# Branch a and c merge logits and all eight gates in Strassen pairs after the convolution, kept in DRAM; branch b merged head by head

## The chip, the cores and the metric

The kernel runs on one core of one Trainium2 chip. The metric is the device time of one execution in microseconds (us). The engines are called as in the profile: PE is the matrix engine, DVE the vector engine, ACT the scalar engine, POOL the general engine (GpSimd), and SP the engine that issues all DMAs of this kernel.

## The reference

One step of a two-layer trunk over 640 tokens (128 context, 512 latent) with 1024 features. Each layer projects the normalised input with one wide matrix, runs three token mixers next to each other, and merges them with a sigmoid gate per channel:

```python
hmod = _rmsnorm(x, norm_g) * (1.0 + scale) + shift
(qa, ka, va, ga, z, xbc, dt_raw, qc, kc, vc, gc, merge) = split(hmod @ w_in)
# a: differential attention, 4 heads   b: Mamba-2 SSD, both directions   c: neighbourhood attention, 8 heads
ma, mb, mc = jnp.split(jax.nn.sigmoid(merge_logits), 3, axis=-1)          # 3 x 1024 logits per token
merged = (ma * ((ya * silu(ga)) @ w_br_a) + mb * (yb @ w_br_b)
          + mc * ((yc * silu(gc)) @ w_br_c))
x = x + gate * (merged @ w_out)
```

The gates `ga` and `gc` have 512 features each; `xbc` goes through a depthwise convolution of five taps before the SSD.

## The kernel before

Features lie on the 128 partitions and tokens on the free axis. Every float32 operand of a large product is kept as a rounded high part and a low rest, and a product is three matmuls (high by high, high by low, low by high). The normalised input is `self.h`, eight pairs of tiles of 128 features by 640 tokens. `feat` computes 128 output features for 640 tokens: two halves of 320 tokens, eight tiles of the contraction, three matmuls each, so 48 matmuls of 128x128 by 320 columns. Its weights come through `weights`: one DMA of 512 KB, a rounding copy on ACT (line 144) and a subtraction on DVE (line 145). `tok` does the same with tokens on the partitions, for values and for z.

A layer runs in five stages. In the convolution stage (`ssd`, lines 562 to 624) PE makes six tiles `xbc`, DVE runs five taps over each (line 609) and the SiLU (line 614), and PE transposes the result (lines 619 and 621). The SSD stage follows: z and dt by `tok`, then the scan in chunks, which writes branch b's output into `self.y`. Then come differential attention (`diff_kq`, `diff_attn`, one head after the other), neighbourhood attention (`na_vkq`, `na_ctx`, `na_head`, two heads at a time), and the tail with the merges of branch c, the output projection and the next norm.

The merge logits are made by `logit`, 48 matmuls for each of 24 tiles per layer, with a tanh, and `logits` spills them to the DRAM tensor `thd`. `merges` reads them back and multiplies them with the branch projection of `self.y`. The tables L1, LA, L2, LC say next to which head the logits of a and c are computed, MA where the merges of branch a stand; all merges of branch b stand at head 0. `gate_in` computes one gate tile (48 matmuls) for each head of a and each pair of heads of c.

A scheduler sets the order of instructions on each engine. It walks the program with priorities in program order and its own idea of each instruction's length, and takes what is ready and has a buffer. On the chip each engine then runs its own list strictly in that order. PSUM has three buffers `mm` for projections; the scores `s` of differential attention have one buffer of three banks, those of neighbourhood attention two.

## Time and profile before

| what | value |
|---|---|
| median of 3 runs | 1656.31 us (1655.13 to 1660.32) |
| the profiled execution | 1660.38 us, its span 1658.6 us |
| PE busy | 1598.4 us, 96% of the span |
| DVE busy | 1061.9 us, 64% |
| ACT busy | 770.3 us, 46% |
| POOL busy | 153.5 us, 9% |
| share of the chain that ended last | PE 79%, DMA 9%, DVE 5%, ACT 3% |

The profile is one execution on the chip. A matmul's record covers its whole passage through the array, so records of neighbouring matmuls overlap and the distance between starts is what one costs. The clock column is the granted clock of PE as a share of 2.4 GHz: 1.00 is 2.4 GHz, 0.50 is 1.2 GHz. Instruction lines (L170) are those of the kernel before.

### The profile page before, as it was taken

How to read it: one execution, taken by the hardware profiler on the slowest of the kernel's cores; microseconds unless marked ns; L12 is line 12 of the kernel's file. 1: busy time of each engine (PE TensorE's matmuls, PEld its weight loads, DVE VectorE, ACT ScalarE, POOL GpSimd, SP SyncE). 2: the span in 40 equal slices, each digit the busy share in tenths (PEclk: the TensorE clock that was granted, in tenths of full speed). 3: DMA queues.
4: the chain of work that ended last, by engine and by line, in shares of the span. 5: the costliest groups of instructions: out<-in, count | busy, mean ns of one | idle time of the engine just before them, and what ended most of it. 6: DMA issues, size and time to landing. Idle time of an engine off the chain costs nothing.

```text
span 1658.6 us, 28802 instructions
## 1 busy us (share of the span) xinstructions
PE 1598.4 (96%) x11166; PEld 1502.9 (91%) x11166; DVE 1061.9 (64%) x2287; ACT 770.3 (46%) x1776; POOL 153.5 (9%) x170
## 2 busy tenths in 40 slices
PE   4999999999999999999999999999999999999997
PEld 2998898999989888889989989999999898999997
DVE  4886767657536565566688668766665374667565
ACT  3647633345445454443456565334444354554432
POOL 0005210101000000000000242201010000000000
PEclk9999999999999999999999999999999999999998
DMA  9422235322265745557542222352222846445553
GB/s 304 124 86 74 83 124 159 99 79 79 75 121 138 159 129 148 165 189 270 172 138 85 82 82 86 118 190 69 72 85 76 158 139 122 111 126 167 198 165 128
DMA packets 114824, 214.61 MB, mean 129 GB/s; under 512 B 36736, under 2 KB 52608, under 8 KB 114688
## 3 DMA queue, kind: packets, MB, share of 16 engines
q1 hardware_dynamic: 114688, 212.78, 44.1%
q8 instruction: 88, 1.44, 0.4%
q14 instruction: 48, 0.39, 0.1%
HBM read 170.27 MB, written 34.08 MB: 123 GB/s over the span
## 4 chain that ended last, share of the span: by engine, by line
PE 79%; DMA 9%; DVE 5%; ACT 3%; issue 3%; SPq 1%; POOL 1%; POOLq 0%; DVEq 0%; ACTq 0%
PE mm L170 54%; PE mm L182 7%; DMA raw<-in_w_feat 2%; PE s L908 2%; PE t L924 2%; PE o L932 2%; PE o L493 2%; PE ada L242 1%; DMA qd<-qr 1%; PE s L478 1%; DMA aw<-in_w_ada 1%; DVE lo L145 1%; PE g L735 1%; ACT hi L144 1%; PE y L748 1%
## 5 line engine op out<-in xcount | busy, mean ns | idle before, releaser
L170 PE MATMUL mm<-hh,hi 128*128 128x320 f32 x1856 | 579.6, 313 | 4.4 <-ACT hh L317 4.4
L170 PE MATMUL mm<-hl,hi 128*128 128x320 f32 x1856 | 580.0, 313 | 2.2 <-DVE hl L318 2.2
L170 PE MATMUL mm<-hh,lo 128*128 128x320 f32 x1856 | 576.0, 311 | 0.5 <-DVE lo L145 0.5
L170 PEld LDWEIGHTS mm<-hh,hi 128*128 128x128 f32 x1856 | 351.0, 189 | 22.4 <-issue 11.5
L170 PEld LDWEIGHTS mm<-hl,hi 128*128 128x128 f32 x1856 | 350.8, 189 | 9.8 <-DVE hl L318 3.6
L170 PEld LDWEIGHTS mm<-hh,lo 128*128 128x128 f32 x1856 | 351.2, 189 | 6.4 <-issue 4.1
L145 DVE TENSOR_TENSOR lo<-raw,hi 128x1024 fp32r<-128x1024 f32 (+2 forms) x194 | 234.4, 1209 | 147.0 <-ACT hi L144 145.3
L144 ACT ACTIVATE hi<-raw 128x1024 fp32r<-128x1024 f32 (+2 forms) x194 | 200.1, 1033 | 231.2 <-PE mm L170 120.2
L170 PE MATMUL mm<-yh,hi 128*128 128x320 f32 x384 | 120.7, 316 | 7.3 <-DVE th L976 5.6
L170 PE MATMUL mm<-yl,hi 128*128 128x320 f32 x384 | 120.1, 313 | 0.2 <-DVE yl L338 0.2
L170 PE MATMUL mm<-yh,lo 128*128 128x320 f32 x384 | 119.1, 310 | 0.0
L487 ACT ACTIVATE ph<-t 128x384 fp32r<-128x384 f32 x64 | 31.3, 488 | 128.3 <-PE t L485 128.3
L182 PE MATMUL mm<-hi,hl 128*128 128x264 f32 (+1 forms) x320 | 90.7, 284 | 0.0
L182 PE MATMUL mm<-lo,hh 128*128 128x264 f32 (+1 forms) x320 | 90.6, 284 | 0.0
L182 PE MATMUL mm<-hi,hh 128*128 128x264 f32 (+1 forms) x320 | 90.4, 284 | 0.1
L170 PEld LDWEIGHTS mm<-yh,hi 128*128 128x128 f32 x384 | 72.7, 190 | 12.2 <-DVE th L976 7.6
L170 PE MATMUL mm<-mgl,hi 128*128 128x320 f32 x256 | 78.6, 308 | 0.0
L170 PE MATMUL mm<-mgh,lo 128*128 128x320 f32 x256 | 78.3, 308 | 0.1
L170 PE MATMUL mm<-mgh,hi 128*128 128x320 f32 x256 | 77.4, 306 | 0.0
L437 DVE TENSOR_REDUCE st<-s 128x2 f32<-128x1536 f32 (+1 forms) x40 | 59.5, 1487 | 26.0 <-PE s L478 24.9
L170 PEld LDWEIGHTS mm<-yl,hi 128*128 128x128 f32 x384 | 73.0, 190 | 0.8 <-DVE yl L338 0.4
L170 PEld LDWEIGHTS mm<-yh,lo 128*128 128x128 f32 x384 | 73.2, 191 | 0.0
(286 smaller groups left out, 2893.0 us busy)
## 6 DMA issues: line engine op xcount, KB each, us to landing
raw<-in_w_feat SPq DMA_DIRECT2D x110, 512.0 KB, 3.7
raw<-in_w_ada SPq DMA_DIRECT2D x32, 512.0 KB, 4.2
raw<-in_w_out SPq DMA_DIRECT2D x32, 512.0 KB, 3.7
thd<-th SPq DMA_DIRECT2D x48, 320.0 KB, 2.2
th<-thd SPq DMA_DIRECT2D x48, 320.0 KB, 3.8
raw<-in_w_br SPq DMA_DIRECT2D x24, 512.0 KB, 3.5
accd<-th SPq DMA_DIRECT2D x32, 320.0 KB, 3.5
ac<-accd SPq DMA_DIRECT2D x32, 320.0 KB, 4.6
```

What stands on the lines that cost most here:

```text
L144: nc.scalar.activation(hi, raw, AF.Copy)
L145: nc.vector.tensor_tensor(out=lo, in0=raw, in1=hi, op=ALU.subtract)
L170: nc.tensor.matmul(ps, lhsT=s, rhs=r, start=(k == 0 and n == 0), stop=(k == K - 1 and n == 2))
L182: nc.tensor.matmul(ps, lhsT=s, rhs=r, start=(k == 0 and q == 0), stop=(k == 7 and q == 2))
L242: nc.tensor.matmul(ps[32 * g:32 * g + 32, :], lhsT=self.sc[:, k, :], rhs=raw[:, 256 * g:256 * g + 256], start=(k == 0), stop=(k == 7))
L437: nc.vector.tensor_reduce(out=st[:, 0:2], in_=s, axis=AX.X, op=ALU.max)
L478: nc.tensor.matmul(s[:, m * 768 + c0:m * 768 + c0 + 512], lhsT=q[:, qs], rhs=ks[m][:, c0:c0 + 512], start=(i == 0), stop=(i == 1))
L487: nc.scalar.activation(ph[dst], pt[:, 0:3, :], AF.Copy)
L493: nc.tensor.matmul(ov[:, 0:256], lhsT=x[:, kt, sv], rhs=q[:, kt, :], start=(kt == 0 and n == 0), stop=(kt == 5 and n == 2))
L908: nc.tensor.matmul(s[:, c0:c0 + n], lhsT=q[:, i * 128:(i + 1) * 128], rhs=ks[j][:, k0:k0 + n], start=(x == 0), stop=(x == 1))
L924: nc.tensor.transpose(pt[:, t, :], e[:, t * 128:(t + 1) * 128], self.ident)
L932: nc.tensor.matmul(out, lhsT=lw, rhs=sel(q), start=(first and x == 0), stop=(last and x == 1))
```

## The change

Two logit tiles or gate tiles at a time are computed by Strassen's seven half-size products. The 2x2 blocks are the two feature tiles by the two halves of the contraction, and the two halves of tokens. `combine` builds, once per layer, the four combinations of `self.h` that the products need: `self.ut` (in the buffers of `self.y`) and `self.u2`. `pair` makes seven products of 12 matmuls each for two tiles, where before two calls of `feat` made 96 matmuls. Its weights are combined on DVE (lines 361 to 363 of the new file) and split in seven blocks; the products accumulate in three PSUM banks, with sums in between on DVE (lines 402, 408 and 412).

`ahead` makes all pairs of a layer in one go, 16 logit tiles of a and c and 8 gate tiles. It is called in `ssd`, behind the convolution and before z. The results go to `thd`, which has a fourth part for gates. `gate_in` now loads a gate from there. The tables L1, LA, L2, LC and their calls are gone. The merges of branch b are spread over the heads of differential attention by MB, two tiles at each. Since the merges of b now read `self.y` until head 3, the four outputs of branch a are held and written to `self.y` together (`last`). The SSD pool moves to the left side of SBUF, and the pool of the values `dv` opens behind `ahead`.

```diff
-L1 = (0,)
-LA = ((), (1, 2), (3,), (4, 5, 6, 7))
-L2 = ()
-LC = ((0,), (1,), (2, 3), (4, 5, 6, 7))
+MB = ((0,), (1,), (2,), (3,))
 MA = ((0,), (), (1,), (2, 3))
...
-        self.feat(self.w_in(l, c), self.h, evac)
+        self.dma(th, self.thd[3, i])
         return th
+
+    def combine(self, p):
+        self.ut = self.y
+        self.u2 = [tuple(p.tile([128, NT], F32R, name=f"u{s}{k}") for s in "hl") for k in range(4)]
+        for k in range(4):
+            f = []
+            for q in (k, k + 4):
+                hi, lo = self.h[q]
+                t = self.stage.tile([128, NT], F32, tag="ac", name="hf")
+                nc.gpsimd.tensor_tensor(out=t, in0=hi.bitcast(F32), in1=lo.bitcast(F32), op=ALU.add)
+                f.append((t[:, 0:320], t[:, 320:640]))
+            c = p.tile([128, 4, 512], F32, tag="sum", name="comb")...
+            u1, t3, u2, t4 = c[:, 0, 0:320], c[:, 0, 320:640], c[:, 1, 0:320], c[:, 1, 320:640]
+            nc.vector.tensor_tensor(out=u1, in0=f[0][0], in1=f[0][1], op=ALU.subtract)
+            nc.vector.tensor_tensor(out=t3, in0=f[1][1], in1=f[0][1], op=ALU.subtract)
+            nc.vector.scalar_tensor_tensor(out=u2, in0=u1, scalar=-1.0, in1=f[1][1], op0=ALU.mult, op1=ALU.subtract)
+            nc.vector.scalar_tensor_tensor(out=t4, in0=u2, scalar=-1.0, in1=f[1][0], op0=ALU.mult, op1=ALU.subtract)
+            for i, (hi, lo) in enumerate((self.ut[k], self.u2[k])):
+                nc.scalar.activation(hi, c[:, i], AF.Copy)
+                nc.vector.tensor_tensor(out=lo, in0=c[:, i], in1=hi, op=ALU.subtract)
+
+    def pair(self, l, c0, c1, p, done):
...
+        a00, a10, a01, a11 = (raw[:, i] for i in range(4))
+        sm = p.tile([128, 4, 512], F32, tag="sum", name="sum")
+        nc.vector.tensor_tensor(out=sm[:, 0:2], in0=raw[:, 0::3], in1=a01..., op=ALU.add)
+        nc.vector.tensor_tensor(out=sm[:, 2], in0=a00, in1=sm[:, 1], op=ALU.add)
+        nc.vector.tensor_tensor(out=sm[:, 3], in0=a10, in1=sm[:, 2], op=ALU.add)
...
+        product(b1, w1, self.h[0:4], lo_t, start=True)
+        p1 = copy("p1", b1)
+        product(b3, w5, self.ut, lo_t, start=True)
+        p5 = copy("p5", b3)
+        product(b2, w6, self.u2, lo_t, start=True)
+        nc.vector.tensor_tensor(out=b2, in0=b2, in1=p1, op=ALU.add)
+        u = copy("p6", b2)
+        product(b1, w2, self.h[4:8], lo_t, stop=True)
+        done(0, 0, b1, 1)
+        product(b2, w7, self.ut, hi_t)
+        nc.vector.tensor_tensor(out=c22, in0=b2, in1=p5, op=ALU.add)
+        done(1, 1, c22, -1)
+        product(b3, w3, self.h[4:8], hi_t, stop=True)
+        nc.vector.tensor_tensor(out=c12, in0=b3, in1=u, op=ALU.add)
+        done(0, 1, c12, 1)
+        product(b2, w4, self.u2, hi_t, stop=True)
+        done(1, 0, b2, -1)
...
             self.pre_end.close()
+            self.ahead(l)
+            vp = outer.enter_context(self.pool("dv"))
             p = es.enter_context(self.pool("ssd2"))
...
-                                if h == 0:
-                                    self.merges(l, 1, range(4), accd, first=True, spilled=range(8))
-                                g = self.gate_in(l, CA_G + 128 * h, cp)
-                                self.logits(l, 0, LA[h])
+                                self.merges(l, 1, MB[h], accd, first=True, spilled=range(8))
+                                g = self.gate_in(h, cp)
...
-                            g = self.gate_in(l, CC_G + 128 * hp, cp)
-                            self.logits(l, 2, LC[hp])
+                            g = self.gate_in(4 + hp, cp)
                             self.na_out(l, hp, y, g)
```

The order of instructions changes at three places. First PE (and DVE) at the end of layer 0's convolution. `hh` and `hl` are tiles of `self.h`, `t` and `g` the PSUM banks of the convolution's transposes. PE before:

```order
L170 MATMUL mm<-hl_96,hi 128x320
L170 MATMUL mm<-hh_95,lo 128x320
L619 MATMUL t<-masks,v 128x128 x4
L621 MATMUL g<-masks,v 128x128
L182 MATMUL mm<-hi,hh_81 128x264
L182 MATMUL mm<-lo,hh_81 128x264
L182 MATMUL mm<-hi,hl_82 128x264
L182 MATMUL mm<-hi,hh_83 128x264
```

PE in the changed kernel, from the first transposes on:

```order
L724 MATMUL t<-masks,v 128x128 x4
L726 MATMUL g<-masks,v 128x128
L724 MATMUL t<-masks,v 128x128 x4
L726 MATMUL g<-masks,v 128x128
L724 MATMUL t<-masks,v 128x128 x4
L726 MATMUL g<-masks,v 128x128
L724 MATMUL t<-masks,v 128x128 x4
L726 MATMUL g<-masks,v 128x128
L821 MATMUL w<-cf,bf 128x128 x2
L724 MATMUL t<-masks,bf 128x128 x4
L726 MATMUL g<-masks,bf 128x128
L386 MATMUL mm<-hh_81,hi 128x320
```

The projection of z (L182) stood between the transposes and now stands behind all twelve pairs. DVE in the changed kernel at the same place, where L719 ends the convolution and `comb` is the buffer of `combine`:

```order
L719 SCALAR_TENSOR_TENSOR v<-cth,v 128x640
L719 SCALAR_TENSOR_TENSOR bf<-cth,bf 128x640
L719 SCALAR_TENSOR_TENSOR cf<-cth,cf 128x640
L344 TENSOR_TENSOR comb<-hf 128x320
L345 TENSOR_TENSOR comb<-hf 128x320
L346 SCALAR_TENSOR_TENSOR comb<-comb,hf 128x320
L347 SCALAR_TENSOR_TENSOR comb<-comb,hf 128x320
L350 TENSOR_TENSOR yl_98<-comb,yh_97 128x640
L350 TENSOR_TENSOR ul_1073<-comb,uh_1072 128x640
L344 TENSOR_TENSOR comb<-hf 128x320
```

`combine` stands behind the convolution's last instruction, in both layers. The second place is PE in head 1 of differential attention in layer 0, behind one tile's scores `s`. Before:

```order
L478 MATMUL s<-ks,qh 128x512
L478 MATMUL s<-ks,ql 128x512
L170 MATMUL mm<-hh_93,hi 128x320
L170 MATMUL mm<-hl_94,hi 128x320
L170 MATMUL mm<-hh_93,lo 128x320
L170 MATMUL mm<-hh_95,hi 128x320
L170 MATMUL mm<-hl_96,hi 128x320
L170 MATMUL mm<-hh_95,lo 128x320
L170 MATMUL mm<-hh_81,hi 128x320
L170 MATMUL mm<-hl_82,hi 128x320
L170 MATMUL mm<-hh_81,lo 128x320
L485 MATMUL t<-masks,e 128x128 x3
```

Changed (L584 is the old L478, L591 the old L485; `rr` and `px` belong to the head's norm and context):

```order
L584 MATMUL s<-ks,qh 128x512
L584 MATMUL s<-ks,ql 128x512
L591 MATMUL t<-masks,e 128x128 x6
L624 MATMUL o<-masks,rr 10x128
L566 MATMUL o<-px,vx 128x128
L580 MATMUL s<-ks,qh 128x256
L580 MATMUL s<-ks,ql 128x256
L584 MATMUL s<-ks,qh 128x512
```

The projections between one tile's scores and the next one's are gone there. The third place is PE at the end of neighbourhood attention in layer 0, where `t` are transposes of the last tiles' weights `e` and `o` is the product with the values. Before:

```order
L170 MATMUL mm<-hh_93,hi 128x320
L924 MATMUL t<-masks,e 128x128 x4
L170 MATMUL mm<-hl_94,hi 128x320
L170 MATMUL mm<-hh_93,lo 128x320
L170 MATMUL mm<-hh_95,hi 128x320
L170 MATMUL mm<-hl_96,hi 128x320
```

Changed (L1016 is the old L908, L1032 the old L924, L1040 the old L932):

```order
L1040 MATMUL o<-pl,vs 128x128
L1016 MATMUL s<-ks,qh 128x128
L1016 MATMUL s<-ks,ql 128x128
L1016 MATMUL s<-ks,qh 128x128
L1016 MATMUL s<-ks,ql 128x128
L1016 MATMUL s<-ks,qh 128x256
L1016 MATMUL s<-ks,ql 128x256
L1032 MATMUL t<-masks,e 128x128 x16
L1040 MATMUL o<-ph,vs 128x512
```

The last head's transposes and scores follow each other with no projection between them.

## Rows read from the trace of the kernel before

**Rows 1.** Busy time of each engine in stretches; stretch, its length, busy (instructions), clock.
```profile
core 0: us, PE busy (x) PEld busy (x) DVE busy (x) ACT busy (x) POOL busy (x), PEclk, DMA share, GB/s
82.00:110.00 28.00, 28.00 (x234) 28.00 (x233) 26.12 (x59) 14.12 (x27) 0.00 (x0) 1.00 0.29 86
...
265.00:505.00 240.00, 231.51 (x1596) 220.06 (x1595) 140.19 (x262) 99.57 (x210) 21.16 (x15) 0.99 0.41 107
505.00:765.00 260.00, 254.35 (x1815) 231.57 (x1815) 148.88 (x381) 121.16 (x310) 1.58 (x1) 0.99 0.55 153
```
**Rows 2.** PE in order of time, end of xbc in layer 0; start, us, instruction.
```profile
81.62 0.31 PE L170 MATMUL mm<-hl,hi 128*128 128x320 f32 x1
81.76 0.31 PE L170 MATMUL mm<-hh,lo 128*128 128x320 f32 x1
81.91 0.60 PE L619 MATMUL t<-masks,v 128*128 128x128 f32 x4
```
**Rows 3.** The same for layer 1.
```profile
896.91 0.28 PE L182 MATMUL mm<-hi,hh 128*128 128x264 f32 x1
```
**Rows 4.** DVE's busy time on line 609 alone, layer 0 and layer 1.
```profile
83.00:110.00 27.00, 15.54 (x31) 1.00 0.29 88
897.00:912.00 15.00, 7.01 (x13) 1.00 0.18 54
```
**Rows 5.** The same for line 614.
```profile
83.00:110.00 27.00, 3.46 (x5) 1.00 0.29 88
897.00:912.00 15.00, 2.94 (x4) 1.00 0.18 54
```
**Rows 6.** Groups by line and shape: busy us, mean ns of one, idle before.
```profile
L286 DVE TENSOR_TENSOR acc<-acc,sq 128x320 f32<-128x320 f32 x42 | 20.5, 488 | 6.5 <-ACT sq L285 5.3
L338 DVE TENSOR_TENSOR yl<-of,yh 128x640 fp32r<-128x640 f32 x8 | 6.5, 818 | 4.5 <-ACT yh L337 4.5
L145 DVE TENSOR_TENSOR lo<-raw,hi 128x1024 fp32r<-128x1024 f32 x174 | 216.2, 1243 | 142.7 <-ACT hi L144 141.1 <-DMA accd<-th 0.9
L337 ACT ACTIVATE yh<-of 128x640 fp32r<-128x640 f32 x8 | 5.9, 740 | 11.9 <-POOL of L532 11.9
L144 ACT ACTIVATE hi<-raw 128x1024 fp32r<-128x1024 f32 x174 | 183.9, 1058 | 216.8 <-PE mm L170 108.5 <-DMA raw<-in_w_feat 66.2 <-DMA raw<-in_w_out 28.8
L532 POOL TENSOR_TENSOR of<-of,gate 128x640 f32<-128x640 f32 x8 | 16.8, 2104 | 95.1 <-ACT hi L144 67.0 <-DVE of L531 28.1
```
**Rows 7.** All engines in order of time, one tile's scores and softmax, differential attention.
```profile
408.54 0.91 ACT L440 ACTIVATE e<-s,st 128x768 f32<-128x768 f32 x1
...
410.09 1.02 DVE L444 SCALAR_TENSOR_TENSOR e<-e,st 128x768 f32<-128x768 f32 x1
...
413.61 0.28 PE L474 MATMUL s<-ks,qh 128*128 128x256 f32 x1
...
415.12 0.40 PE L478 MATMUL s<-ks,ql 128*128 128x512 f32 x1
415.56 1.76 DVE L437 TENSOR_REDUCE st<-s 128x2 f32<-128x1536 f32 x1 [3.25 <-PE s L478]
```
**Rows 8.** Groups by line and shape: softmax of neighbourhood attention on DVE.
```profile
L926 DVE TENSOR_TENSOR pl<-t,ph 128x512 fp32r<-128x512 f32 x64 | 43.6, 681 | 12.2 <-ACT ph L925 12.2
L921 DVE TENSOR_SCALAR e<-e,st 128x512 f32<-128x512 f32 x64 | 31.1, 486 | 1.9
L912 DVE CUSTOM_DVE_ANT_0 e<-s,bias 128x256 f32<-128x256 f32 x64 | 27.0, 421 | 46.7 <-PE t L924 27.9 <-PE t L889 10.6 <-PE s L908 7.8
L919 DVE TENSOR_TENSOR st<-st 128x1 f32<-128x1 f32 x64 | 10.1, 158 | 36.0 <-ACT e L918 35.3
```
**Rows 9.** Stretches of 5 us around one of PE's waits for a DMA.
```profile
1295.00:1300.00 5.00, 2.40 (x18) 1.99 (x17) 0.56 (x1) 2.79 (x11) 0.00 (x0) 0.96 1.07 181
1300.00:1305.00 5.00, 4.85 (x22) 4.04 (x23) 0.00 (x0) 0.00 (x0) 0.00 (x0) 0.50 1.42 103
1305.00:1310.00 5.00, 5.00 (x34) 4.99 (x34) 1.88 (x3) 2.79 (x6) 0.00 (x0) 0.85 1.22 162
```

More of the change, by code (lines that the diff above doesn't have):

```diff
@@ L319, in norm_part, with gate_in @@
                                                op1=ALU.subtract)
-    def gate_in(self, l, c, p):
-        nc = self.nc
-        th = p.tile([128, NT], F32, tag="gate", name="gate")
-        def evac(half, ps):
-            t = th[:, half * 320:half * 320 + 320]
-            nc.scalar.activation(t, ps, AF.Tanh, scale=0.5)
-            nc.vector.scalar_tensor_tensor(out=t, in0=t, scalar=1.0, in1=ps, op0=ALU.add, op1=ALU.mult)
-        self.feat(self.w_in(l, c), self.h, evac)
-        return th
+    def gate_in(self, i, p):
+        th = p.tile([128, NT], F32, tag="gate", name="gate")
+        self.dma(th, self.thd[3, i])
+        return th
@@ new lines, in combine @@
+    def combine(self, p):
+        nc = self.nc
+        self.ut = self.y
[7 more added lines that the diff above has]
+                f.append((t[:, 0:320], t[:, 320:640]))
+            c = p.tile([128, 4, 512], F32, tag="sum", name="comb").rearrange("p a n -> p (a n)")[:, 0:2 * NT]
+            c = c.rearrange("p (a n) -> p a n", a=2)
+            u1, t3, u2, t4 = c[:, 0, 0:320], c[:, 0, 320:640], c[:, 1, 0:320], c[:, 1, 320:640]
[6 more added lines that the diff above has]
+                nc.vector.tensor_tensor(out=lo, in0=c[:, i], in1=hi, op=ALU.subtract)
@@ new lines, in ahead, with done @@
+    def ahead(self, l):
+        nc = self.nc
+        with self.pool("ahead") as p:
+            self.combine(p)
+            jobs = [(C_M + 1024 * b + 128 * m, self.thd[b, m], 0) for b in (0, 2) for m in range(8)]
+            jobs += [(c + 128 * h, self.thd[3, o + h], 1) for c, o in ((CA_G, 0), (CC_G, 4)) for h in range(4)]
+            for i in range(0, len(jobs), 2):
+                ab = jobs[i:i + 2]
+                th = [self.stage.tile([128, NT], F32, tag="th", name="th") for _ in ab]
+                def done(m, half, v, sign):
+                    t = th[m][:, half * 320:half * 320 + 320]
+                    if ab[m][2]:
+                        nc.scalar.activation(t, v, AF.Tanh, scale=0.5)
+                        nc.vector.scalar_tensor_tensor(out=t, in0=t, scalar=1.0 * sign, in1=v, op0=ALU.add, op1=ALU.mult)
+                    else:
+                        nc.scalar.activation(t, v, AF.Tanh, scale=0.5 * sign)
+                self.pair(l, ab[0][0], ab[1][0], p, done)
+                for m in range(2):
+                    self.dma(ab[m][1], th[m])
@@ L533, in diff_out, with ssd @@
         self.dump(f"ya{l}_{h}", of)
-        self.put_y(h, of)
-    def ssd(self, l):
+    def ssd(self, l, outer):
         nc, a, o, sm = self.nc, self.a, self.o, self.sm
         with ExitStack() as es:
-            p = es.enter_context(self.pool("ssd"))
+            p = es.enter_context(self.pool("ssd", side="left"))
             pa = es.enter_context(self.pool("ps_a", space=PSUM))
@@ L783, in ssd @@
                     nc.vector.tensor_tensor(out=lo[:, tk], in0=yf[:, m], in1=hi[:, tk], op=ALU.subtract)
+            return vp
     def na_vkq(self, l, hp, p, pp, after_v=lambda: None):
@@ L1027, in build @@
             accd = dram.tile([8, 128, NT], F32, name="accd")
-            self.thd = dram.tile([3, 8, 128, NT], F32, name="thd")
+            self.thd = dram.tile([4, 8, 128, NT], F32, name="thd")
             src = a["x"]
@@ L1033, in build @@
             self.pre_end = ExitStack()
-            pre = self.pre_end.enter_context(self.pool("pre", side="left"))
+            pre = self.pre_end.enter_context(self.pool("pre"))
             with self.pool("x0") as xp, self.pool("aw0", bufs=9) as wp, self.pool("ps_a0", space=PSUM) as pp:
@@ L1066, in build @@
                 with ExitStack() as ph:
-                    with self.pool("dv") as vp:
-                        self.ssd(l)
+                    with ExitStack() as dv:
+                        vp = self.ssd(l, dv)
                         cp = ph.enter_context(self.pool("carry", side="left"))
@@ L1072, in build @@
                         self.logits(l, 1, range(8))
-                        self.logits(l, 0, L1)
                         with self.pool("diff") as p, self.pool("ps_d", space=PSUM) as ps:
@@ L1076, in build @@
                             kq = self.diff_kq(l, 0, p)
-                            pend = []
+                            pend, outs = [], []
                             for h in range(4):
@@ L1088, in build, with last @@
                                 d = self.diff_norm(att, cp, pp)
+                                outs.append(att[0])
                                 pend.append(lambda h=h, att=att, d=d, g=g: self.diff_out(l, h, att, d, g, sg, pp))
-                    self.logits(l, 2, L2)
                     with self.pool("na") as p, self.pool("ps_n", space=PSUM) as ps:
-                        vkq = self.na_vkq(l, 0, p, pp, lambda: pend and pend.pop()())
+                        def last():
+                            pend.pop()()
+                            for h in range(4):
+                                self.put_y(h, outs[h])
+                        vkq = self.na_vkq(l, 0, p, pp, last)
                         ys, gate, nxt = [], [], []
```

36 lines of the change are left out of this document (added).

## The prediction

> **What bounds the kernel now.** I read the busy times by stretch first. PE is busy in 28.00 of 28 us at the end of layer 0's convolution, in 231.51 of 240 us of differential attention and in 254.35 of 260 us of neighbourhood attention [rows 1]; DVE, the next one, has 140.19 and 148.88 us in the two attention stretches, under 60%. The kernel is bound by PE because every wait for DVE or ACT has a projection matmul standing in PE's list behind it. Then I read PE in order of time: neighbouring matmuls of 320 columns start 0.14 to 0.15 us apart [rows 2]; I take 0.146. Last I read what DVE does where the change takes PE's cover away.
>
> **What it removes.** A pair of tiles took 96 matmuls and takes 84. There are 12 pairs in a layer and two layers, so 24 x 12 = 288 matmuls go, 288 x 0.146 = **42 us** at most, all on the path. The splits move with them and grow: per pair seven blocks of 512 columns instead of four, plus the sums, about 8.4 us of DVE (3.5 x 1.24 for the low parts, 2.6 for the weight sums, three adds of 0.49 [rows 6]) beside 84 x 0.146 = 12.3 us of PE. DVE holds that pace, so this work alone is hidden by the pair's own matmuls.
>
> **What it moves, 1: the end of the convolution.** In the old order z's matmuls follow at once when the last xbc matmul is done, at 81.9 us in layer 0 [rows 2] and 896.9 us in layer 1 [rows 3]. In the new order only the convolution's transposes follow, and behind them the pairs, whose products with `ut` and `u2` need `combine`. On DVE `combine` stands behind the last convolution instruction. So PE waits for DVE's rest of the convolution, then for `combine`, then for the first weight sums.
>
> The rest of the convolution: after 83 us DVE still spends 15.54 + 3.46 = 19.0 us on it [rows 4, 5], in layer 1 after 897 us 7.01 + 2.94 = 10.0 us. Neighbouring records overlap a little, and z's splits no longer stand between, so I put its end at 101 us (99 to 103) and 905.5 us (904 to 908).
>
> `combine` has four rounds. A round needs two POOL adds of 640 columns; the nearest row is a POOL product of the same size, 2.10 us [rows 6]. Their buffers come free only when DVE has read the round before, so a round lasts about 2 x 2.1 = 4.2 us. Its DVE part (four operations of 0.49, two of 0.82) and ACT's 0.74 end 3 us behind the second add. Three rounds, 12.6, plus the last one's 4.2 make 17 us with the first adds partly hidden; then the weight sums (1.24 + 0.7) and their split (1.06), 3 us. In all 20 us (16 to 23) from the convolution's end to full pace. The Trainium skill (SBUF — State Buffer, "SBUF: two separate sides") says that POOL and a two-input DVE operation lock each other out of a shared port for a whole instruction. No run here shows POOL's add without DVE beside it; by that rule adds and DVE work would follow each other in a round of some 6 us, an estimate that would make the sum 7 us a layer longer.
>
> PE's work inside: five groups of transposes of about 0.45 us from the first start to the next instruction [estimated from rows 2: four start within 0.43], and the first pair's 24 products with `h`, 3.5 us; 6 us. So PE stands still for 101 + 20 - 82 - 6 = **33 us** in layer 0 and 905.5 + 20 - 897 - 6 = **23 us** in layer 1, together +56 (44 to 66). Nothing is gained back: z still has to be made afterwards, and the SSD scan begins only then.
>
> **The clock after that.** After a wait of 2.6 us before (5 us with 2.40 busy) the granted clock is 0.50, the level of 1.2 GHz, in the next 5 us and 0.85 in those behind [rows 9], a loss of 2.5 + 0.8 = 3.3 us. Part of it falls into the 24 products that wait anyway. Two times 2: +4 (0 to 8).
>
> **2: hand-overs inside the pairs.** Product 7 is added into the bank into which DVE has just added p1 and from which ACT copied p6; one or two products (1.75 or 3.5 us) stand between. The two operations take 0.5 + 0.4 us, but each can stand behind a split (1.24, 1.06 [rows 6]): 3.2 us. So 0 to 1.5 us per pair; the order of PE leaves two products between in half of the cases, I take 0.4: +10 (0 to 36).
>
> **3: differential attention without filler.** With gates and logits gone it has 4 x 48 + 7 x 48 = 528 matmuls less per layer, counted above as moved. What is left in PE's list is not spread: the projections for the next head all stand in heads 0 and 2, and heads 1 and 3 run nearly bare. Scores have one buffer, so the next tile's scores start when both exponentials have read it: scores 1.4 us (413.61 to 415.12 with three transposes between), the maximum 1.76, a small operation 0.2, two exponentials 2 x 0.9, hand-overs about 0.3 [rows 7], 5.5 us. PE's own work in a cycle is 1.4 of scores, 0.65 of transposes and 9 value matmuls of 256 columns, 1.05 (by 0.146 for 320): 3.1. Idle 2.4. The new list has six cycles per layer without filler (three in head 1, three in head 3), two context parts of 1.4, and at the end of head 3 the softmax and the last value product, about 6. With some waiting of DVE's list inside: **23 us** per layer, +46 (24 to 64).
>
> **4: neighbourhood attention without filler.** 576 matmuls less per layer. Per tile DVE takes 0.42 twice, 0.49, 0.68 and four small ones of 0.16 to 0.2 [rows 8], 2.6 us; PE 0.47 of scores, 0.43 of transposes, 0.47 of values, 1.4. Where no projection stands between, that is 1.2 idle per tile. In the new list about 14 of 32 tiles of a layer are bare, all eight of the last pair of heads among them, 17 us; then the chain from the last scores over the value product, the sum, the gate and `put_y` to branch c's merges, which need the last tile of `self.y`, some 6 us bare. 23 per layer, less 5 us of adaLN matmuls that stand in these gaps in layer 0 and the waits that the old kernel has anyway: +38 (16 to 60). Behind the new waits stand, on SP, the loads of weights in the same list as the gate loads; they are early, so I give them nothing.
>
> **The sum.** -42 + 56 + 4 + 10 + 46 + 38 = +112 on the profiled execution's 1660.4 us, 1772. The median of the runs is 4 us below that execution, so I predict **1768 us**.
>
> **Rivals.** *Only the convolution costs.* If DVE and ACT run the bare attention tiles faster than I read, or the remaining projections slip under them, terms 3 and 4 vanish: -42 + 56 + 4 = +18, 1674 us, with hand-overs up to 1690. Against it: the list has no projection in those places, and PE can't leave its list. For it: DVE is under 60% busy there. 12%.
>
> *The clock stays low.* In bare stretches PE works 3.1 of 5.5 us and 1.4 of 2.6. If it is held at 1.2 GHz there as in [rows 9], scores (1.4) and transposes take twice as long: +1.5 in the 12 bare cycles of both layers, +0.8 in the 28 bare tiles, and some 10 for the projections next to them that run slower too, together +50: 1818 us. The Trainium skill (TensorE: Matmul & The Clock Gate, "HAM oscillation — how this bites in real kernels") says that matmuls in bursts with waits between fall back to the low clock burst after burst, a rule against this change. The trace shows it once per long wait, and shows none for waits of 1 us. 18%.
>
> *Faster.* The 42 us arrive if `combine` runs under the xbc matmuls instead of behind the convolution: its inputs are ready, only its buffers and its place in the list hold it. Then the wait is DVE's convolution rest alone, 19 + 8 us less the 6 us of PE's work in each, some 16 us, and with bare attention hidden it would be -42 + 16 + 10 = -16, 1640 us. It decides below a wait of 42 us in sum. The list speaks against it: in both layers `comb` stands behind L719. 4%. That fewer matmuls are made than I count is no rival: the PE lists have 10697 and 10409 instructions of this kind.
>
> **How the numbers follow.** The forecast holds 66%. The range has to leave out no more than 2 in 10: from all terms near their low ends (-42 + 44 + 24 + 16 = +42, 1698) up to all but the last of the low-clock rival, 1835. So 1700 to 1835. A measurement tells 0.3%, about 5 us, from no change. Faster 0.04 (the last rival), the same 0.03 (the first rival with its wait at the low end), slower 0.93.
>
> **What would show it.** Right: PE idle for 25 to 40 us behind xbc in layer 0 and somewhat less in layer 1, ended by DVE's sums or ACT's split; PE waits for ACT's exponentials and DVE's or ACT's softmax in heads 1 and 3 and in the last pair of heads; the twelve pairs in 147 us a layer plus a few. Wrong: pairs that run well over 160 us (hand-overs), attention stretches that shrink by the full 77 and 84 us per layer (528 and 576 matmuls), or a busy PE between xbc and the first pair.

## The result and the profile after

The changed kernel takes 1869.85 us (median of 4 runs, 1865.44 to 1875.78) against 1658.32 us before (4 runs, 1655.13 to 1661.49): a ratio of 1.1278, 95% interval 1.1233 to 1.1323. Its profiled execution spans 1863.6 us, 205.0 us more than before. PE's page entry went from 1598.4 to 1640.7 us busy, although it makes 288 matmuls fewer (x11166 to x10878).

The windows view of the changed kernel, by stage: the end of the convolution with the pairs and the scan, differential attention, neighbourhood attention, first layer 0, then layer 1. Columns as in [rows 1].

```profile
82.40:418.80 336.40, 301.08 (x2065) 286.83 (x2064) 241.76 (x390) 173.21 (x370) 58.34 (x46) 0.94 0.29 99
418.80:635.10 216.30, 186.16 (x1155) 169.02 (x1153) 143.49 (x292) 85.50 (x182) 24.14 (x22) 0.87 0.29 88
635.10:872.20 237.10, 206.84 (x1363) 178.67 (x1362) 136.24 (x373) 107.20 (x295) 2.74 (x2) 0.90 0.61 152
997.40:1335.70 338.30, 311.58 (x2125) 297.46 (x2124) 240.13 (x389) 176.17 (x376) 58.61 (x46) 0.94 0.29 98
1335.70:1548.30 212.60, 181.79 (x1155) 165.77 (x1153) 145.03 (x291) 85.38 (x182) 24.97 (x22) 0.90 0.29 89
1548.30:1765.30 217.00, 186.94 (x1231) 169.18 (x1230) 135.54 (x368) 106.11 (x293) 2.74 (x2) 0.93 0.53 128
```

The same six stages of the kernel before, cut at the same instructions (bounds that [rows 1] doesn't have).

```profile
81.90:229.50 147.60, 147.60 (x1058) 136.37 (x1057) 109.03 (x231) 87.41 (x230) 41.07 (x38) 1.00 0.27 85
229.50:484.80 255.30, 249.44 (x1722) 238.67 (x1721) 161.88 (x312) 105.58 (x216) 28.03 (x22) 0.99 0.34 104
484.80:763.90 279.10, 270.82 (x1921) 246.66 (x1921) 154.33 (x393) 128.34 (x331) 2.75 (x2) 0.99 0.60 153
886.40:1043.40 157.00, 157.00 (x1122) 145.90 (x1121) 110.35 (x229) 90.56 (x237) 41.89 (x38) 1.00 0.26 81
1043.40:1297.50 254.10, 249.25 (x1722) 238.49 (x1720) 161.24 (x311) 105.53 (x216) 29.12 (x22) 0.99 0.34 104
1297.50:1560.50 263.00, 258.40 (x1806) 246.28 (x1807) 155.61 (x388) 127.62 (x329) 3.51 (x2) 0.98 0.54 133
```

Two things are to be read off. Length less busy time is PE's idle time: from 0 to 35.3 and 26.7 us in the first stage, from 5.9 and 4.9 to 30.1 and 30.8 us in differential attention, from 8.3 and 4.6 to 30.3 and 30.1 us in neighbourhood attention. And the busy time is longer than the matmuls in it: differential attention of layer 0 has 567 matmuls fewer, at 0.146 us 82.8 us, so 249.44 - 82.8 = 166.7 us were to be left, and it is 186.16. This excess is 19.5 and 15.3 us there, 17.5 and 12.5 us in neighbourhood attention, 6.5 and 8.1 us in the first stage. The clock column tells why: 0.87 to 0.94 where it was 0.98 to 1.00. A stage at 0.87 spent 2 x 0.13 = 26% of its time at the level of 1.2 GHz, 56 us of the 216.3 in differential attention of layer 0. PE was busy in 86% of that stage, and half of 0.86 x 56 is 24 us: an estimate from the clock column alone, near the 19.5 us of excess.

What PE waited for over the whole span (the waits view: us in total, times, longest):

```profile
PE mm L386 <- ACT hi L371: 29.9, 4, 11.4
PE t L724 <- DVE v L719: 23.1, 4, 12.8
...
PE t L1032 <- DVE st L1023: 14.1, 9, 2.5
PE t L591 <- DVE pl L594: 12.2, 8, 2.0
```

The first two are the end of the convolution; the others are transposes of attention that wait for the softmax or for the transposes ahead of them to be read. At the full clock the pairs run without a gap: in a stretch of 20 us inside them PE is busy 20.00 us with 140 matmuls, 0.143 us each.

```profile
145.00:165.00 20.00, 20.00 (x140) 20.00 (x139) 12.67 (x17) 10.23 (x20) 0.00 (x0) 1.00 0.49 171
```

### The profile page after: what moved, and what is told of

The parts are those of the page before. It is cut to its first block, busy times and chain, and to the rows that moved or that the text cites. A ratio compares the mean times of both kernels' runs of the same rounds, so it can differ in the third digit from the quotient of the medians.

```text
span 1863.6 us, 28849 instructions
## 1 busy us (share of the span) xinstructions
PE 1640.7 (88%) x10878; PEld 1518.3 (81%) x10878; DVE 1249.9 (67%) x2527; ACT 855.6 (46%) x1912; POOL 178.7 (10%) x186
## 5 line engine op out<-in xcount | busy, mean ns | idle before, releaser
L167 PE MATMUL mm<-hh,hi 128*128 128x320 f32 x1088 | 343.2, 316 | 8.6 <-ACT hh L314 4.5
L167 PE MATMUL mm<-hl,hi 128*128 128x320 f32 x1088 | 343.7, 316 | 2.1 <-DVE hl L315 2.1
L167 PE MATMUL mm<-hh,lo 128*128 128x320 f32 x1088 | 339.4, 312 | 0.2 <-DVE lo L142 0.2
L142 DVE TENSOR_TENSOR lo<-raw,hi 128x1024 fp32r<-128x1024 f32 (+2 forms) x146 | 176.2, 1208 | 85.1 <-ACT hi L141 83.9
L167 PEld LDWEIGHTS mm<-hh,hi 128*128 128x128 f32 x1088 | 208.6, 192 | 20.2 <-issue 5.9
L141 ACT ACTIVATE hi<-raw 128x1024 fp32r<-128x1024 f32 (+2 forms) x146 | 149.5, 1026 | 146.3 <-PE mm L167 62.6
L167 PEld LDWEIGHTS mm<-hl,hi 128*128 128x128 f32 x1088 | 208.4, 192 | 10.1 <-issue 3.9
L167 PEld LDWEIGHTS mm<-hh,lo 128*128 128x128 f32 x1088 | 208.5, 192 | 3.4 <-issue 1.5
L167 PE MATMUL mm<-yh,hi 128*128 128x320 f32 x384 | 120.4, 317 | 7.3 <-ACT yh L443 6.6
L386 PE MATMUL mm<-hh,hi 128*128 128x320 f32 x288 | 90.2, 313 | 8.9 <-ACT hi L371 7.1
L386 PE MATMUL mm<-hh,lo 128*128 128x320 f32 x288 | 90.2, 314 | 5.4 <-DVE lo L372 5.4
L386 PE MATMUL mm<-hl,hi 128*128 128x320 f32 x288 | 90.8, 316 | 0.0
L386 PE MATMUL mm<-yh,hi 128*128 128x320 f32 x192 | 60.6, 315 | 22.8 <-ACT hi L371 22.8
L371 ACT ACTIVATE hi<-sum 128x1024 fp32r<-128x1024 f32 x48 | 50.8, 1062 | 61.5 <-PE mm L386 54.8
L167 PE MATMUL mm<-mgl,hi 128*128 128x320 f32 x256 | 78.6, 308 | 0.0
```

Of the source, the lines that this page charges most:

```text
L141: nc.scalar.activation(hi, raw, AF.Copy)
L142: nc.vector.tensor_tensor(out=lo, in0=raw, in1=hi, op=ALU.subtract)
L167: nc.tensor.matmul(ps, lhsT=s, rhs=r, start=(k == 0 and n == 0), stop=(k == K - 1 and n == 2))
L371: nc.scalar.activation(hi, src, AF.Copy)
L386: nc.tensor.matmul(ps, lhsT=s, rhs=r, start=(start and k == 0 and n == 0), stop=(stop and k == 3 and n == 2), skip_group_check=True)
```

## The experiments

**Theory**, after these two traces: attention lost its filler (idle time, and a slow clock because of it), and `combine` is late; the pairs themselves are fine. **Rivals**: the pairs cost more than their matmuls; the merges by head do the harm; the excess of busy time isn't the clock. Medians are set against 1869.85 us; intervals are those of the ratio to the kernel before.

### The attention's filler: c_only and a_only

`c_only` gives the tiles of a back to differential attention, `a_only` those of c to neighbourhood attention.

```diff
-jobs = [... for b in (0, 2) for m in range(8)]
-jobs += [... for c, o in ((CA_G, 0), (CC_G, 4)) for h in range(4)]
+jobs = [... for b in (2,) for m in range(8)]
+jobs += [... for c, o in ((CC_G, 4),) for h in range(4)]
...
-g = self.gate_in(h, cp)
+g = self.gate(l, CA_G + 128 * h, cp)
+self.logits(l, 0, LA[h])
```

> The changed kernel with the logits of a and the four gates of a computed beside differential attention again, by 48 plain matmuls each and next to the same heads as in the kernel before; only the logits and gates of c are made in pairs behind the convolution (six pairs a layer instead of twelve). Merges of b stay spread over the heads. Theory: differential attention has its filler back, so its extra idle time (24.3 and 25.9 us) and its slow clock (19.5 and 15.3 us) go, 85 us, against 144 matmuls more, 21 us: about 1806 us (1790 to 1825). Rival: the loss in differential attention comes from spreading the merges of b over the heads: then nothing comes back and it is 1870 to 1890 us.

> The changed kernel with the logits and gates of c computed beside neighbourhood attention again, 48 plain matmuls each, next to the same pairs of heads as in the kernel before; only those of a are made in pairs behind the convolution (six pairs a layer). It is the counterpart of the run that gave a's back, which went from 1870 to 1796 us. Theory: neighbourhood attention gets back its extra idle time (22 and 25.5 us) and slow clock (17.5 and 12.5 us), 77 us, against 144 matmuls more, 21 us: 1813 us (1800 to 1830). Rival: neighbourhood attention is bound by its own chains also with the filler, since its tiles keep one buffer of transposes: 1850 us or more.

`c_only` took 1796.12 us (1.0745 to 1.0853), 74 us less; `a_only` 1807.71 us (1.0832 to 1.0936), 62 us less. The stage that got its tiles back, layer 0, first of `c_only` (differential), then of `a_only` (neighbourhood):

```profile
347.50:593.40 245.90, 240.07 (x1654) 230.61 (x1653) 159.27 (x311) 104.76 (x215) 26.43 (x22) 0.99 0.31 99
```

```profile
564.00:845.70 281.70, 272.03 (x1914) 248.16 (x1915) 154.26 (x393) 128.03 (x332) 2.74 (x2) 0.98 0.59 151
```

Idle time is back at 5.8 and 9.7 us, the clock at 0.99 and 0.98. Each run also makes 144 matmuls more (21 us), so the lost filler had cost 95 and 83 us. The traces alone gave 85 and 77.5 us (idle and excess together). For both stages it is shown that the lost filler is the cause.

### Strassen or the place: plain_ahead

```diff
-            self.combine(p)
...
-                self.pair(l, ab[0][0], ab[1][0], p, done)
+            self.feat(self.w_in(l, c), self.h, evac)
```

> The changed kernel without Strassen: the 24 tiles are still made behind the convolution, ahead of z, and kept in DRAM, but each by 48 plain matmuls, so combine and the pairs are gone. The rest (merges of b by head, attention without filler) is as in the changed kernel. Theory: 288 matmuls more (+42 us), while PE no longer waits at the end of the convolution, since the plain tiles need only self.h (62 us of waits and some 14 us of slow clock back): about 1835 us (1820 to 1850); what is left over the kernel before, about 175 us, is the attention stages alone. Rival: the pairs themselves cost more than their 84 matmuls (hand-overs between the seven products, DVE's seven splits): then it comes out below 1810 us.

1843.15 us (1.1034 to 1.1134). PE is idle for 1.7 us from the last xbc matmul to the end of the scan:

```profile
83.30:399.50 316.20, 314.46 (x2210) 302.89 (x2209) 147.24 (x272) 131.16 (x301) 43.03 (x38) 1.00 0.35 107
```

So moving the tiles costs 183 us without any Strassen, and Strassen, put in there, made it 27 us worse in place of 42 us better: its waits and their slow clock (62 + 15 us) eat the saving.

### The end of the convolution: z_first, combine_dve, spread_combine

```diff
+            for i in range(2):   # z_first: z's projections
+                w = [self.weights(a["w_z"][l, i, e], 4, 264) for e in range(2)]
+                ...
             self.ahead(l)
...
-                nc.gpsimd.tensor_tensor(out=t, in0=hi.bitcast(F32), ...)   # combine_dve
+                nc.vector.tensor_tensor(out=t, in0=hi.bitcast(F32), ...)
...
+            for c, dst, gate in jobs[:6]:   # spread_combine: both edits above, and
+                self.feat(self.w_in(l, c), self.h, evac)
+                self.dma(dst, t6)
+                next(rounds, None)          # one round of combine
```

> The changed kernel with one thing moved: z's and dt's projections stand ahead of the pairs again, as they stood behind the convolution in the kernel before. Nothing else differs. Theory: the end of the convolution costs what PE stands still there, 35.3 us in layer 0 and 26.7 us in layer 1, and some 14 us for the slow clock in the pairs behind it; z's 240 matmuls per layer cover DVE's rest of the convolution and the combination of self.h, so about 70 us come back: 1800 us (1790 to 1815), with PE busy from the last xbc matmul to the first pair. Rival: the wait is only put off, since z's splits and sums stand on DVE between the convolution and the combination, so the pairs wait then: 1830 to 1865 us with a wait of 10 us or more behind z.

1839.71 us (1.1025 to 1.1122): 30 us came back, not 70. The rival held. PE's waits from 80 to 300 us:

```profile
PE mm L386 <- ACT hi L371: 13.2, 2, 12.5
```

Why `combine` is still late there is seen in the changed kernel too. Its round in order of time (start, duration):

```profile
103.08 0.48 DVE L344 TENSOR_TENSOR comb<-hf 128x320 f32<-128x320 f32 x1
...
104.05 1.72 POOL L339 TENSOR_TENSOR hf<-hh,hl 128x640 f32<-128x640 f32 x1 [3.20 <-DVE comb L345]
104.41 1.71 DVE L347 SCALAR_TENSOR_TENSOR comb<-comb,hf 128x320 f32<-128x320 f32 x1
106.04 0.81 DVE L350 TENSOR_TENSOR yl<-comb,yh 128x640 fp32r<-128x640 f32 x1
106.26 1.99 POOL L339 TENSOR_TENSOR hf<-hh,hl 128x640 f32<-128x640 f32 x1 [0.50 <-DVE comb L347]
106.92 2.01 DVE L350 TENSOR_TENSOR ul<-comb,uh 128x640 fp32r<-128x640 f32 x1
109.04 0.49 DVE L344 TENSOR_TENSOR comb<-hf 128x320 f32<-128x320 f32 x1
...
110.25 3.16 DVE L372 TENSOR_TENSOR lo<-raw,hi 128x1024 fp32r<-128x1024 f32 x2
...
117.35 0.49 DVE L344 TENSOR_TENSOR comb<-hf 128x320 f32<-128x320 f32 x1
...
123.30 0.49 DVE L344 TENSOR_TENSOR comb<-hf 128x320 f32<-128x320 f32 x1
...
126.78 1.23 DVE L361 TENSOR_TENSOR sum<-raw 128x1024 f32<-128x1024 f32 x1
...
128.77 2.01 ACT L371 ACTIVATE hi<-sum 128x1024 fp32r<-128x1024 f32 x2 [2.88 <-DVE sum L362]
```

A DVE operation that starts while a POOL add runs ends only behind the add: L347 takes 1.71 us instead of 0.48 and ends 0.35 us after the add of 104.05, L350 takes 2.01 instead of 0.81 and ends 0.68 us after the add of 106.26. The first round is 109.04 - 103.08 = 5.96 us, not 4.2. The four rounds take 5.96, 8.31, 5.95 and 3.48 us: the splits of the first pair's weights (L372) stand on DVE inside the second, and no add stands beside the last. So the split of the first weight sums, which PE waits for, starts 25.7 us behind the convolution's end at 103.1 us. The prediction cited the Trainium skill for this (SBUF — State Buffer, "SBUF: two separate sides": a POOL instruction and a two-input DVE operation hold a shared port against each other for a whole instruction). The trace agrees with it, by the ends of L347 and L350 above.

> The changed kernel with the eight adds of hi and lo in combine on DVE instead of POOL. In the trace of the changed kernel DVE's small operations last 1.7 and 2.0 us instead of 0.5 and 0.8 whenever a POOL add runs. Theory: POOL's add and DVE's operations shut each other out, so a round takes about 6 us; on DVE alone a round is 2 x 0.8 + 4 x 0.49 + 2 x 0.82 = 5.2 us, without hand-overs, so PE's first product with ut comes some 3 to 5 us earlier in each layer: 1860 to 1866 us. Rival: DVE is the engine that is late there, and adds of its own make it later by 6.4 us a layer: 1876 to 1883 us.

1867.27 us (1.1199 to 1.1278). The first product with `ut` starts at 125.2 us in layer 0, 4.7 us earlier than in the changed kernel (129.9), as the theory has it, but the interval overlaps that of the changed kernel and the median lies outside the theory's range, so a gain in time isn't shown. Neither is the rival's loss.

> The changed kernel with z ahead of the pairs, combine's adds on DVE, and the first six tiles (logits of a) by 48 plain matmuls each, one behind each of combine's rounds, so nine pairs a layer instead of twelve. Theory: with z alone moved, combine still ran behind z for some 30 us, six to seven us a round, and the pairs waited 12.5 us at once; here plain tiles cover the rounds, so no wait above 2 us is left between xbc and the last pair. Against the changed kernel: 62 us of waits and 14 us of slow clock less, 3 pairs a layer by 12 matmuls of 0.146 us more, 10.5 us: 1804 us (1795 to 1820). Rival: DVE stays late all through the pairs, since its splits of the plain tiles stand among the rounds: 1820 us or more with waits for DVE of 10 us or more.

1818.90 us (1.0921 to 1.0995), 51 us less, at the upper end of the theory's range. The rival's sign, waits for DVE, is absent:

```profile
82.00:170.00 88.00, 88.00 (x655) 87.68 (x654) 67.53 (x119) 41.44 (x74) 0.00 (x0) 1.00 0.38 129
170.00:272.00 102.00, 102.00 (x714) 101.96 (x713) 68.89 (x97) 52.15 (x90) 1.05 (x1) 1.00 0.35 120
```

PE stands still for no moment from xbc to the last pair, at a clock of 1.00. Put so, nine pairs a layer are 24 us faster than plain tiles (18 pairs x 1.75 = 31.5 us by the matmuls). The two runs differ also in z's place, but the gain stands where the pairs are: from the convolution's first transposes to the first maximum of differential attention (the TENSOR_REDUCE on `s`) this run takes 306.6 and 314.5 us in the two layers, `plain_ahead` 320.1 and 325.4, together 24.4 us more. The waits were `combine`'s; the pairs hold their pace.

### Do the two losses add: c_spread

Both edits, `c_only` and `spread_combine`, at once.

> Two edits at once: a's logits and gates beside differential attention again (alone 1870 to 1796 us), and z ahead of the pairs with combine's rounds on DVE among six plain tiles (alone 1870 to 1819 us); what is left for Strassen is three pairs of c a layer. Theory: the losses at the end of the convolution and in differential attention are separate, so the gains add: 1870 - 74 - 51 = 1745 us (1735 to 1757). Rival: one wait covers the other (what one edit gives back is lost again behind it): 1760 us or more.

1736.98 us (1.0396 to 1.0512). They add (1745 expected). The rest above the kernel before is for the most part neighbourhood attention's: in layer 0 PE is idle for 30.6 us between 635 and 860 us of this run, at a clock of 0.92, and for 3.3 and 7.6 us in the two stretches before it (82.6 to 389 and 389 to 635 us), at 1.00 and 0.99.

### Merges by head: merges_head0

```diff
-self.merges(l, 1, MB[h], accd, first=True, spilled=range(8))
+if h == 0:
+    self.merges(l, 1, range(4), accd, first=True, spilled=range(8))
```

> The changed kernel with all merges of b at head 0 again, as in the kernel before; nothing else differs. 144 matmuls of a layer (21 us) move from behind heads 1 to 3 to head 0. Theory: they are filler, and where they leave, a bare stretch gets longer by what they covered, while head 0 had enough: 10 to 30 us slower, 1880 to 1900 us. Rival: merges by head are what makes differential attention slow (held outputs, reads of self.y until head 3): then it gets faster by 20 us or more.

1869.64 us (1.1212 to 1.1294): no difference, and neither side was right. Merges by head are not the cause, and their 21 us of matmuls are worth no less at head 0 than spread over the heads.

### The clock: fill_idle, fill_few, fill_gap

Extra matmuls into the bank of the next transposes, in heads 1 and 3 and in the bare tiles of neighbourhood attention (`fill_few`: 5 and 3 in place of 14 and 7; `fill_gap`: 14 and 6 of 128 columns behind the transposes).

```diff
+                spare = pp.tile([128, 4, 128], F32, tag="t", name="t")
+                if j:
+                    self.idle(14, spare, qh[1][:, qs])
                 e = soft(...)
```

> The changed kernel with 392 extra matmuls of 320 columns whose results nobody reads (14 behind each tile's scores in heads 1 and 3 of differential attention, 7 behind each tile's scores in the fourth and the last two heads of neighbourhood attention); the order of everything else is the same. At 0.146 us they are 57 us of PE work. Theory: they stand in PE's idle time and cost nothing, and the excess of busy time in the attention stages (19.5 and 15.3 us in differential, 17.5 and 12.5 us in neighbourhood attention, against the matmuls that are left) is the clock's half level behind idle time, of which most comes back: 1830 us (1810 to 1850) with the granted clock in the stretches of heads 1 and 3 near 1.00 instead of 0.65 to 0.83. Rival: the excess comes from something else (matmuls that stream slower next to DVE's and ACT's reading of PSUM): no time comes back, 1870 us, up to 1925 us where the extra matmuls delay the next step.

1878.38 us (1.1254 to 1.1383): nothing came back, the rival's number, but not its reason. Five stretches of 10 us around head 1 in the changed kernel, then in this run:

```profile
490.00:500.00 10.00, 7.80 (x35) 6.66 (x33) 5.13 (x9) 2.21 (x9) 0.00 (x0) 0.66 0.00 0
500.00:510.00 10.00, 5.95 (x27) 4.69 (x27) 5.88 (x16) 4.54 (x11) 1.18 (x1) 0.77 0.01 2
510.00:520.00 10.00, 9.21 (x47) 7.44 (x47) 5.24 (x9) 2.47 (x7) 0.71 (x1) 0.71 0.04 13
520.00:530.00 10.00, 4.96 (x34) 3.76 (x33) 6.32 (x13) 4.48 (x11) 0.87 (x1) 0.80 0.12 34
530.00:540.00 10.00, 7.69 (x35) 6.48 (x36) 5.26 (x13) 3.89 (x13) 0.00 (x0) 0.69 0.01 2
```

```profile
490.00:500.00 10.00, 8.87 (x42) 7.73 (x41) 3.98 (x8) 3.68 (x12) 0.00 (x0) 0.66 0.01 2
500.00:510.00 10.00, 7.11 (x42) 6.29 (x41) 7.12 (x17) 4.12 (x11) 1.18 (x1) 0.87 0.01 3
510.00:520.00 10.00, 10.00 (x69) 9.01 (x68) 4.20 (x9) 2.88 (x7) 1.56 (x1) 0.96 0.05 15
520.00:530.00 10.00, 6.84 (x38) 6.13 (x37) 5.74 (x10) 2.99 (x7) 0.00 (x0) 0.89 0.10 32
530.00:540.00 10.00, 7.28 (x46) 5.78 (x45) 5.76 (x14) 4.10 (x14) 0.00 (x0) 0.94 0.00 0
```

The clock rose from a mean of 0.73 to 0.86, and what it does on the path is seen at one tile's eight score matmuls (L580 and L584 of the changed kernel, first start to the transposes behind them), 2.73 us in the changed kernel and 1.48 us here:

```profile
498.30 1.76 DVE L543 TENSOR_REDUCE st<-s 128x2 f32<-128x1536 f32 x1 [2.40 <-PE s L584]
...
502.47 0.58 PE L580 MATMUL s<-ks,qh 128*128 128x256 f32 x1 [0.49 <-ACT e L546]
...
505.20 0.63 PE L591 MATMUL t<-masks,e 128*128 128x128 f32 x3
...
505.44 1.76 DVE L543 TENSOR_REDUCE st<-s 128x2 f32<-128x1536 f32 x1 [1.33 <-PE s L584]
```

```profile
501.79 0.36 PE L585 MATMUL s<-ks,qh 128*128 128x256 f32 x1
...
503.27 0.49 PE L599 MATMUL t<-masks,e 128*128 128x128 f32 x3
...
507.87 3.60 PE L173 MATMUL t<-hh,qh 128*128 128x320 f32 x14
...
511.31 0.28 PE L585 MATMUL s<-ks,qh 128*128 128x256 f32 x1
```

The cycle from one tile's maximum (L543) to the next one's is 505.44 - 498.30 = 7.14 us in the changed kernel. Here it is 6.59 us, 0.55 less, since the scores also begin later behind the maximum (4.91 us, against 4.17). In the next cycle the 14 extra matmuls (L173, 3.60 us) stand ahead of the scores and take back what was won.

> The changed kernel with extra matmuls at the same places as in the run with 392, but 5 behind a tile's scores of differential attention and 3 in neighbourhood attention: 2 x (40 + 36) = 152 extra matmuls, 22 us at the full clock. In the run with 392 the granted clock came back to 0.87 to 1.00 in the bare stretches, but they kept their length: one cycle from maximum to maximum went from 7.14 to 6.59 us, in the next the extra matmuls themselves (3.60 us) held up the scores. Theory A: the half clock costs time on the path; with fewer extra matmuls in the way and a clock of 0.9 or more the bare stretches get shorter: 1835 to 1860 us. Theory B: DVE's and ACT's chain sets the pace of a bare tile whatever PE's clock is, and the excess of busy time is PE's waiting time turned into slower work: 1865 to 1875 us whatever the clock is.

1874.63 us (1.1233 to 1.1320), inside theory B's range. But the mean clock of the run is 0.924 (0.922 without the extra matmuls), and 0.80 in the same five stretches around head 1 (0.73): the clock didn't reach the 0.9 that theory A asks for, so this run can't tell A from B.

> The changed kernel with extra matmuls of 128 columns, whose results nobody reads, between the two groups of three transposes of a tile (14) and behind the second group (6), in heads 1 and 3 of differential attention: 2 layers x 8 tiles x 20 = 320 of them, where PE waits for the first group to be read. In the run with 392 extra matmuls the clock came back but some of them stood ahead of the next scores and held them up by 1.7 us; three cycles where they didn't were 0.55, 2.1 and 1.2 us shorter than in the changed kernel (6.59, 5.13 and 5.68 against 7.14, 7.23 and 6.92 us). Theory: at the full clock a bare cycle costs about 1.3 us less, since scores and transposes stand on its chain; over some 10 bare cycles a layer that is 2 x 10 x 1.3 = 26 us: 1845 us (1838 to 1858), the rest of the loss in differential attention stays. Rival: DVE's and ACT's part of the chain alone sets the pace: 1866 to 1875 us with a granted clock above 0.9 in the bare stretches.

1899.97 us (1.1403 to 1.1484), 30 us more: a miss. The extra matmuls got onto the chain, since ACT's copy of the transposes waited for them:

```profile
516.58 1.76 PE L172 MATMUL t<-hh,qh 128*128 128x128 f32 x14
518.37 0.49 ACT L600 ACTIVATE ph<-t 128x384 fp32r<-128x384 f32 x1 [7.79 <-PE t L172]
```

16 tiles x 1.76 = 28 us, about the 30 measured. That fits a bare tile's chain setting the time, but isn't shown tile by tile: the groups of six matmuls (0.86 us at one of them) would add up to 14 us more. What stays open: how much of the 65 us of excess in attention the full clock alone would give back. No run raised the clock without putting work on the chain.

### Holding the filler back: even_filler

`spread_combine`, with the loads of attention's remaining projections held until a given tile's softmax is done, so that they stand beside the bare tiles; some merges of a and b move to other heads as well (the tables MA and MB).

```diff
+        if hold is not None:
+            nc.gpsimd.tensor_copy(raw[0:1, 0, 0:1], hold[0:1, 0:1])
         self.dma(raw, src)
```

> The kernel with z first and combine's rounds among plain tiles (1818.9 us, nine pairs a layer), and the weights of the projections that serve as filler in attention are loaded only when a certain tile's softmax is done: K and Q for the next head at two tiles of the head before, the second half of the values in head 1, the merges of b one or two in each of heads 0, 2 and 3, the merges of a in the later heads of neighbourhood attention. So the same projections stand spread over the bare tiles instead of early in the list. The work is the same, but for some 160 copies of one element on POOL. Theory: both attention stages lost time because projections ran early and left tiles bare, not because there are too few: 600 and 624 matmuls a layer are left there, 88 and 91 us, against waits of 10 x 4.8 us and 15 x 2 us a layer. With one or two dozens of matmuls beside each tile the waits and the slow clock go for the most part: 100 of the 154 us come back: 1720 us (1690 to 1750). Rival: the chains of DVE and ACT are too long for what is left, or the held loads come late and PE waits for them: 1790 us or more.

1839.60 us (1.1050 to 1.1116), 21 us slower than `spread_combine`: the rival. PE's waits in attention of layer 0, and one of SP's over the span:

```profile
PE mm L171 <- ACT hi L145: 15.8, 9, 3.0
PE ada L243 <- DMA raw<-in_w_ada: 14.4, 7, 4.1
```

```profile
SPq L132 <- POOL raw L141: 209.8, 38, 23.8
```

The held projections came late (15.8 us; in `spread_combine` that wait isn't among the eleven largest of the stretch, the last of which is 2.6 us), and SP stood at the holds for 209.8 us. A part of that replaced other waits of SP: those for the low-part splits (L146 here, L142 there) went from 308.7 to 217.6 us. That the loads behind the holds came late because of them (14.4 us for adaLN's weights, 4.2 in `spread_combine`) is argued, not tried. No version run here beats the kernel before.

## Why the prediction was right or wrong

The direction and the places of the loss were right; the size was wrong by 93 us: +205.0 against +112 on the profiled execution, and 1870 lies outside the range of 1700 to 1835. Measured, by the two window tables:

| step of the prediction | predicted | measured |
|---|---|---|
| fewer matmuls | -42 | -42 (288 fewer) |
| waits at the convolution's end | +56 | +62.0 (35.3 + 26.7) |
| slow clock there | +4, behind the waits | +14.6 (6.5 + 8.1), in the whole stage |
| hand-overs in pairs | +10 | 0 |
| differential attention, idle | +46 | +50.3 |
| neighbourhood attention, idle | +38 | +47.5 |
| attention, slow clock | 0 in the forecast, 50 as a rival | +64.8 |
| rest of the span | 0 | +7.8 |

**The step that failed** is "The clock stays low" as a rival of 18% and not a term. The prediction priced each wait with the chain at 2.4 GHz and took from [rows 9] that the clock falls once per long wait. PE's waits in differential attention of layer 0, 418.8 to 635.1 us:

```profile
PE t L591 <- DVE pl L594: 6.4, 4, 2.0
PE s L559 <- ACT e L546: 2.8, 2, 2.3
```

No wait of this stretch is longer than 2.3 us, and still the granted clock of head 1 is 0.66 to 0.80. So the matmuls beside the waits ran at the half clock for a large part of the stage, and the busy time of all four attention stretches is 64.8 us longer. It reaches the path: a bare cycle was priced at 5.5 us with 1.4 us of scores, and the one above takes 7.14 us, with 2.97 from the first score matmul (502.47) to the next maximum (505.44). The Trainium skill's rule against this change (TensorE: Matmul & The Clock Gate, "HAM oscillation — how this bites in real kernels": bursts of matmuls with waits between them run at the low clock again and again) described what happened; the trace agrees with it. The Trainium skill's own case there has waits for a DMA that are longer than any wait of this stretch; the low clock beside waits of at most 2.3 us is shown by this trace alone. The mistake was to set the slow clock against the forecast as a rival, while it comes with the same idle time that the forecast holds: their sum was the rival's 1818 us, near the top of the range. Attention was priced at 84 us and lost 162.6, 78.6 more: 64.8 of slow clock and 13.8 of idle time. The convolution's end lost 76.6 us in place of 60, 16.6 more. With 7.8 us of rest, less the 10 us of hand-overs, that is the 93 us. One caveat: idle time and excess are a split of one loss, measured with the slow clock; with a fast one PE would have waited longer for the same DVE and ACT work. How much of the 64.8 us a full clock alone would give back stays open, as said above.

That the idle time of differential attention came so near (50.3 against 46) is partly luck: it was worked out from six bare cycles a layer at the full clock, and the trace has longer ones at the slow clock.

**The convolution's end** was right in place and nearly in size. The term that was too small is the way to full pace, 20 us, where it was 26.8 in layer 0 (103.1 to 129.9 us) and 26.8 in layer 1 (1019.1 to 1045.9 us): 13.6 of the 16.6 us. Of the two values for a round, 4.2 us by rows and 6 us by the shared port, two of the four rounds show the second (5.96 and 5.95 us), and the prediction took the first. That four rounds together came to 23.7 us, near 4 x 6, is partly luck: the second (8.31 us) holds the splits of the first pair's weights, which the prediction put at nothing, and the last (3.48 us) has no add beside it. The clock behind the waits was priced about right: 0.66 from 130 to 135 us and 1.00 in the next 5 us in layer 0, 0.50 from 1045 to 1050 us and 0.84 in the next 5 us in layer 1, which is some 5 us together. The rest of the 14.6 us is PE's work inside the wait, which ran at 0.66 and 0.63 in layer 0 and filled part of the idle time; so that came out only 6 us higher.

**Hand-overs** were priced at 10 us and are none: from 129.9 to 279.3 us PE is busy in all 149.4 us. **"Only the convolution costs"** is refuted by `c_only` and `a_only`, **"Faster"** by the waits: 62 us exceed the 42 at which it decides. Of its own signs, idle time of 25 to 40 us in layer 0 and less in layer 1, ended by ACT's split, and the waits in attention came as written.

## What to carry to other kernels

A projection that stands beside a latency-bound softmax is not only its own matmuls: moved away, 24 tiles a layer cost 183 us here, and of the changed kernel's loss in attention two fifths (65 of 163 us) were the longer busy time of the matmuls left behind, much of it at half the clock. Where a change takes PE's cover away, price the wait and the slow clock together, with scores and transposes at the lower level. And a saving in matmuls counts only where its preparation has cover of its own: `combine` under plain tiles, with z ahead of it, turned a loss of 27 us against plain tiles into a gain of 24.

## What the runs showed of the hardware

A two-input DVE operation of 0.48 us took 1.71 us when it started beside a running POOL add, and ended 0.35 us behind the add. The granted clock had a mean of 0.73 over 50 us (490 to 540 us of the changed kernel) in which no wait of PE was longer than 2.3 us. And in `fill_gap` 14 matmuls of 128 columns, which all name the same weights, took 1.76 us, about 0.12 us each, no less than one of 256 columns in the same trace (0.12 us between starts); PEld loaded the weights 14 times for them (1.64 us).
